# First modulation of a hybrid retention, attention and expert block: in quarters over four column groups

## The chip, the cores and the metric

The kernel runs on one core of a Trainium2 chip. The metric is the device time of one execution in microseconds (us); less is better. The engines are PE (TensorE, matmuls), DVE (VectorE), ACT (ScalarE), POOL (GpSimd) and SP (SyncE, which issues most DMAs). All data are float32.

## What is computed

The block takes 256 latent tokens `x` and 256 context tokens `ctx` of width 1024, a vector `c` for the latent rows and one `c_ctx` for the context rows. What matters here is its beginning:

```python
def ada_mod(cvec, w, b):
    m = jax.nn.silu(cvec) @ w + b          # w is 1024 x 6144
    return jnp.split(m[:, None, :], 6, axis=-1)

def modulate(t, shift, scale):
    return t * (1.0 + scale) + shift

h_lat = modulate(rms_norm(x, norm1_g), m_lat[0], m_lat[1])
h_ctx = modulate(rms_norm(ctx, norm1_g), m_ctx[0], m_ctx[1])
zl = split_proj(h_lat @ w_in)              # w_in is 1024 x 8896
zc = split_proj(h_ctx @ w_in)
```

The first 2048 columns of `ada_w` make shift and scale of this first modulation, for both kinds of rows. Of the projection, 384 columns (the latent query rank, "cq"), 320 columns (the key and value rank with its rotary part, "ckv") and 512 columns of a gate ("gm") are computed first. Retention, attention, the merge of both, 32 experts of which each token takes four, and a last norm follow.

## The kernel before, in words

The program is a list of steps, each a function and, where it needs weights, a load (`step`, `run_steps`, L205 to L250). Weights are loaded by SP into a ring of 7 tiles (`WR`), so a load is issued when the step seven loads earlier has used its tile. Each engine runs its instructions in the order in which the steps were written. A float32 product of a weight block is made of three matmuls (`mm3`, L282): the weights are split into a high part (ACT, L274) and the rest (DVE, L275), and so are the modulated rows, `hh` (ACT, L379) and `hl` (DVE, L381, from `hf`, which DVE or POOL computes, L378).

The beginning, in steps:

- `ada_half(0)`: for each of 8 row blocks k of `ada_w`, one load of 128 rows by 2 x 512 columns (the first 512 shifts and the first 512 scales). Two matmuls with 32 stationary columns (`sT`, of which two are real: silu of `c` and of `c_ctx`), one per column group of PE, add into bank `ap0` (L306). The bias comes as a matmul ahead of the first block (L294).
- Meanwhile the rows of `x` and `ctx` are loaded, squared and summed (ACT, L348), scaled (`norm_rows`, L353, L355) and turned (`xn_transposes`, L143) into `xT`. `keep_warm` (L455) issues small matmuls on ones, of which nothing is used.
- `start1`: `ada_out(0)` copies the sums from `ap0` (L313, L314), `ada_mod(0)` turns them into columns (L320) and makes gain and shift for the first four k (L322, L324); `modulate` follows for those four.
- The cq products for k = 0 to 3, the ckv products for k = 0 and 1, then `ada_half(1)`, 8 more blocks with four small matmuls behind each; `start2` with the same steps for k = 4 to 7; the rest of cq, `cq_norm` (which first clears a 2 MB tile `ada` on POOL, L327), the rest of ckv, `cq_rows` (turning the normed cq, L143), gm, `ckv_norm`, `ckv_rows`, and the gate.

Then the query weights follow in three blocks ("up q", 256 columns moving, on `cqh`), the keys and values (on `ckh`), and the rest.

Of the kernel before, what the change touches and what calls it, by code (L numbers as in the profile page):

```python
# [10 lines left out]
F32 = mybir.dt.float32  # L11
# [23 lines left out]
CLK = 60, 6, 4, 10, 20, 20, 16, 8, 16, 16  # L35
# [24 lines left out]
def hybrid_block(ctx: ExitStack, tc: tile.TileContext, A, out, dbg=None):  # L60
# [135 lines left out]


# [13 lines left out]
    def run_steps():  # L211
# [9 lines left out]
        def split_next():  # L221
            w, nk, n, raw = loaded[len(ready)]
            if raw:
                ready.append((w,))
            else:
                ready.append([y[:, :nk * n].rearrange("p (k n) -> p k n", k=nk) for y in split(w[:, :nk * n], nk * n)])
# [9 lines left out]
        for spec, fn in steps:  # L236
            while len(loaded) < min(at[0] + WR, len(loads) - 1):
# [14 lines left out]
    def load(src, r0, nk, pieces, raw=False):  # L252

        n = sum(p[1] for p in pieces)
        w = wtile4()
        v = w[:, :nk * n].rearrange("p (k n) -> p k n", k=nk)
        o = 0
        if len(pieces) > 1 and len({p[1] for p in pieces}) == 1 and nk == 1:
            (c0, cn), (c1, _) = pieces
            a = src[r0:r0 + 128]  # L260
            a = bass.AP(tensor=a.tensor, offset=a[:, c0:c0 + cn].offset, ap=[list(a.ap[0]), [c1 - c0, 2], [1, cn]])
            nc.sync.dma_start(w[:, :n].rearrange("p (c n) -> p c n", c=2), a)
# [5 lines left out]
        return w, nk, n, raw  # L268
# [24 lines left out]
    def ada_bias(ps, r):  # L293
        nc.tensor.matmul(ps, ident[0:12, r:r + 1].to_broadcast([12, 32]), adab, start=True, stop=False)  # L294

    def ada_half(h, ks):
        for k in ks:
            def f(w, k=k):
                if h == 0 and k == 0:
                    bank("ap0")  # L300
                ap0 = B["ap0"]
                for c in range(2):
                    g = 2 * h + c
                    if k == 0:
                        ada_bias(ap0[32 * g:32 * g + 32], 2 * c + h)
                    nc.tensor.matmul(ap0[32 * g:32 * g + 32], sT[:, k], w[:, 512 * c:512 * c + 512],  # L306
                                     start=False, stop=(k == KD - 1))
            step(f, (A["ada_w"][0], 128 * k, 1, [(512 * h, 512), (1024 + 512 * h, 512)], True))

    def ada_out(h):  # L310
        s = slice(64 * h, 64 * h + 64)
        ap0 = B["ap0"]
        nc.vector.tensor_copy(ada0[s, 0:256], ap0[s, 0:256])  # L313
        nc.scalar.activation(ada0[s, 256:512], ap0[s, 256:512], AF.Copy)  # L314

    def ada_mod(h):
        s = slice(64 * h, 64 * h + 64)
        ps = pt_((128, 4, 2, 32))
        for c in range(4):
            nc.tensor.transpose(ps[:, c].rearrange("p a b -> p (a b)"), ada0[s, 128 * c:128 * c + 128], ident[s, s])  # L320
        ks = slice(4 * h, 4 * h + 4)
        nc.vector.scalar_tensor_tensor(mod1[:, 0, :, ks], ps[:, :, 1, 0:2].rearrange("p k r -> p r k"), 1.0,  # L322
                                       g1c[:, None, ks].to_broadcast([128, 2, 4]), op0=OP.add, op1=OP.mult)
        nc.vector.tensor_copy(mod1[:, 1, :, ks], ps[:, :, 0, 0:2].rearrange("p k r -> p r k"))  # L324
# [4 lines left out]

    ada_todo = [(q, k, i) for q in range(2) for k in range(KD) for i in range(2)]  # L330
# [13 lines left out]
    def norm_rows():  # L344
# [4 lines left out]
        r1 = rsqrt(sp, ss, 4, 1.0 / D)  # L349
# [7 lines left out]
    def xn_transposes(u):  # L357
        for k2 in range(KD // 2):
# [6 lines left out]
            if k2 % 2:  # L365
# [20 lines left out]
    def project(pieces, jobs, kks, mid=None, at=None):  # L386

        for k2 in kks:
            def f(hi, lo, k2=k2):
                for k in range(2):  # L390
                    kk = 2 * k2 + k
                    for n, (name, cut, t, a, b, first) in enumerate(jobs):
# [1337 lines left out]
```

## Time and profile before

| | |
|---|---|
| median of 3 runs | 1474.54 us (1474.64, 1470.18, 1474.54) |
| the profiled execution | 1469.68 us, span of its instructions 1467.8 us |
| PE, DVE, ACT busy | 96%, 44%, 24% of the span |
| DMA | 492 MB, mean 335 GB/s |

The stage in question ends near 92 us. A busy PE is not a PE at its peak: matmuls overlap, and a row's duration is longer than the distance to the next one. Where a cost per matmul is wanted, the distance between starts is read.

### The profile page before, as it was taken

To read this page: it belongs to the slowest core of one execution; us is meant where nothing else is said; L and a number is where in the kernel's file an instruction comes from. 1 tells how busy PE (TensorE), PEld (TensorE's weight loads), DVE (VectorE), ACT (ScalarE), POOL (GpSimd) and SP (SyncE) were. 2 spreads that over 40 slices of the span, in tenths; PEclk is the share of its full clock that TensorE was granted. 3 is DMA by queue.
4 is the path that set the end of the run, shared out by engine and by line. 5 is a ranking of instruction groups with operands and counts; after the bars stand their busy time and mean duration, and the time that the engine had idled before them with its cause. 6 is when DMAs were issued, how large, how long until landed. Compare 5 with 4: busy or idle time off the path is not lost.

```text
span 1467.8 us, 18597 instructions
## 1 busy us (share of the span) xinstructions
PE 1405.6 (96%) x7695; PEld 795.8 (54%) x7695; DVE 648.5 (44%) x1113; ACT 348.3 (24%) x605; POOL 72.2 (5%) x84
## 2 busy tenths in 40 slices
PE   8999999999999999999999999999999899999985
PEld 4688888888888764434334334333433343334333
DVE  4488776868675753233233233232222232223224
ACT  4365633534443431101101101101100011001001
POOL 2200050110101000000000000000000000000000
PEclk9999999999999999999999999999999999999998
DMA  8633372654568789999999999999999999999994
GB/s 289 201 120 106 106 270 84 206 169 162 169 205 319 272 338 422 427 427 427 427 427 427 426 428 426 427 427 426 427 427 427 427 427 427 427 428 427 426 422 166
DMA packets 75075, 492.36 MB, mean 335 GB/s; under 512 B 6579, under 2 KB 16892, under 8 KB 50152
## 3 DMA queue, kind: packets, MB, share of 16 engines
q1 hardware_dynamic: 74008, 489.22, 82.9%
q0 software_dynamic: 576, 1.23, 0.3%
q8 instruction: 62, 1.02, 0.3%
q10 hardware_dynamic: 400, 0.66, 0.1%
q14 instruction: 29, 0.24, 0.0%
HBM read 490.03 MB, written 1.05 MB: 335 GB/s over the span
## 4 chain that ended last, share of the span: by engine, by line
PE 55%; DMA 39%; DVE 4%; ACT 1%; issue 1%; POOL 0%; ACTq 0%; DVEq 0%; SPq 0%
DMA w<-in_exp_w_gu_dram 25%; DMA w<-in_exp_w_down_dram 14%; PE ps L1495 12%; PE ps L284 9%; PE ps L285 9%; PE ps L283 9%; PE ps L1526 6%; PE ps L143 2%; PE ps L1354 2%; PE ps L306 1%; PE ps L1442 1%; PE ps L1475 1%; PE ps L455 1%; DVE ws L275 0%; PE ps L1648 0%
## 5 line engine op out<-in xcount | busy, mean ns | idle before, releaser
L1495 PE MATMUL ps<-w,xg 128*64 128x512 f32 x2048 | 459.7, 596 | 32.3 <-DMA w<-in_exp_w_gu_dram 30.5
L1495 PEld LDWEIGHTS ps<-w,xg 128*64 128x64 f32 x2048 | 141.0, 137 | 329.0 <-issue 255.8
L1526 PE MATMUL ps<-w,ga 128*64 128x512 f32 x992 | 218.1, 592 | 0.0
L1482 DVE SCALAR_TENSOR_TENSOR x<-ps,gate,x 128x512 f32<-128x512 f32 x124 | 84.5, 745 | 183.8 <-PE ps L1475 183.8
L275 DVE TENSOR_TENSOR ws<-w,ws 128x1024 fp32r<-128x1024 f32 (+2 forms) x114 | 139.4, 1231 | 57.7 <-ACT ws L274 56.0
L1526 PEld LDWEIGHTS ps<-w,ga 128*64 128x64 f32 x992 | 71.3, 137 | 141.5 <-issue 141.5
L274 ACT ACTIVATE ws<-w 128x1024 fp32r<-128x1024 f32 (+2 forms) x114 | 116.8, 1028 | 90.0 <-PE ps L285 71.6
L1535 DVE TENSOR_TENSOR ps<-ps,gate 128x512 f32<-128x512 f32 (+1 forms) x33 | 22.5, 683 | 259.3 <-PE ps L1526 250.0
L1500 ACT ACTIVATE ps<-ga 128x512 f32<-128x512 f32 x32 | 19.3, 602 | 467.8 <-DVE ga L1499 467.8
L284 PE MATMUL ps<-ws,hh 128*128 128x512 f32 (+3 forms) x304 | 109.8, 361 | 3.7 <-DVE ws L275 3.7
L283 PE MATMUL ps<-ws,hh 128*128 128x512 f32 (+3 forms) x304 | 110.3, 363 | 0.1
L285 PE MATMUL ps<-ws,hl 128*128 128x512 f32 (+3 forms) x304 | 109.0, 359 | 0.4 <-DVE hl L381 0.4
L1499 DVE TENSOR_SCALAR ga<-ps 128x512 f32<-128x512 f32 x32 | 22.1, 692 | 159.7 <-PE ps L1495 159.7
L279 ACT ACTIVATE up<-ps 128x512 fp32r<-128x512 f32 (+1 forms) x33 | 19.3, 584 | 258.8 <-DVE ps L1535 258.7
L284 PEld LDWEIGHTS ps<-ws,hh 128*128 128x128 f32 x304 | 57.2, 188 | 14.0 <-DVE ws L275 5.6
L283 PEld LDWEIGHTS ps<-ws,hh 128*128 128x128 f32 x304 | 57.1, 188 | 9.1 <-DVE ptl L280 0.3
L285 PEld LDWEIGHTS ps<-ws,hl 128*128 128x128 f32 x304 | 57.1, 188 | 9.1 <-DVE hl L381 0.7
L1354 PE MATMUL ps<-bgu,ident 128*64 128x512 f32 x256 | 62.0, 605 | 0.0
L338 DVE SCALAR_TENSOR_TENSOR ada<-w,sc,ada 128x1024 f32<-128x1024 f32 x32 | 40.9, 1279 | 0.0
L1515 ACT ACTIVATE ga<-ps 128x512 f32<-128x512 f32 x32 | 19.1, 597 | 73.5 <-PE ps L143 73.5
L284 PE MATMUL ps<-atl,hth 128*128 128x256 f32 x128 | 35.8, 280 | 0.7 <-DVE atl L280 0.7
L1442 PE MATMUL ps<-oh,acc_m 128*128 128x128 f32 x256 | 36.4, 285 | 0.0
(381 smaller groups left out, 1839.5 us busy)
## 6 DMA issues: line engine op xcount, KB each, us to landing
w<-in_exp_w_gu_dram SPq DMA_DIRECT2D x124, 2048.0 KB, 39.1
w<-in_exp_w_down_dram SPq DMA_DIRECT2D x62, 2048.0 KB, 39.1
w<-in_ada_w_dram SPq DMA_DIRECT2D x48, 512.0 KB, 5.7
w<-in_w_in_dram SPq DMA_DIRECT2D x48, 512.0 KB, 4.8
w<-in_w_in_dram SPq DMA_DIRECT2D x32, 256.0 KB, 4.3
w<-in_w_branch_ret_dram SPq DMA_DIRECT2D x16, 512.0 KB, 4.9
w<-in_exp_w_gu_dram SPq DMA_DIRECT2D x8, 1024.0 KB, 27.3
w<-in_w_branch_mla_dram SPq DMA_DIRECT2D x8, 512.0 KB, 5.1
```

The source lines that it names most:

```text
L143: nc.tensor.transpose(dst, src, ident[:n, :n])
L274: nc.scalar.activation(hi[:, :n], src, AF.Copy)
L275: nc.vector.tensor_tensor(lo[:, :n], src, hi[:, :n].bitcast(F32), op=OP.subtract)
L283: nc.tensor.matmul(ps, a[0], b[0], start=start, stop=False, skip_group_check=True)
L284: nc.tensor.matmul(ps, a[0], b[1], start=False, stop=False, skip_group_check=True)
L285: nc.tensor.matmul(ps, a[1], b[0], start=False, stop=stop, skip_group_check=True)
L338: nc.vector.scalar_tensor_tensor(a, w, sc[:, k:k + 1], a, op0=OP.mult, op1=OP.add)
L1354: nc.tensor.matmul(ps[64 * h:64 * h + 64], pick_row(c // 512).to_broadcast([128, CAP]), bgu, start=True, stop=False, skip_group_check=True)
L1442: nc.tensor.matmul(ps[:, i, :w], pairs(part[:, t], 4)[:, k // 2, k % 2], rhs, start=(t + p + i == 0), stop=(t + p == 2), skip_group_check= ...
L1482: nc.vector.scalar_tensor_tensor(a, pss[h], g[:, t:t + 1], a, op0=OP.mult, op1=OP.add)
L1495: nc.tensor.matmul(ps[64 * h:64 * h + 64], xg[k // 4][:, k % 4, sl], w[:, c:c + 512], start=False, stop=(k == KD - 1), skip_group_check=True)
L1526: nc.tensor.matmul(py[64 * h:64 * h + 64], hT[f], w[:, 1024 * r + 512 * h:1024 * r + 512 * h + 512], start=(f == 0), stop=(f == KD - 1))
```

## The change

The first modulation is computed in quarters instead of halves. A quarter is 256 shifts and 256 scales, that is two k of the rows. Its 8 row blocks go round four column groups (block kk to group kk % 4) and so leave four partial sums; `sel`, a 128 by 2 matrix of ones and zeros, adds them up in the matmuls that also turn them into columns. The bias is turned into columns once (`bsc`) and added there. Each load still brings 512 KB, now as two DMAs of 256 KB with rows of 256 columns. The first six loads go into tiles that later stages use (`early_tile`), outside the ring of seven. The cq and ckv products for two k stand between the quarters. The split of the first cq weights comes ahead of the scaling of the rows; the turning of the rows goes by k for both kinds; `ada` is cleared at the program's start; `cq_rows` moves behind the first gm block and `ckv_rows` behind the last.

```diff
-CLK = 60, 6, 4, 10, 20, 20, 16, 8, 16, 16
+CLK = 100, 6, 4, 10, 20, 20, 16, 8, 16, 16
...
 (in gain_cols)
+        bp = pt_((128, 4, 16))
+        for j in range(4):
+            transpose(bp[:, j, 0:12], adab[:, 128 * j:128 * j + 128])
+        for h in range(2):
+            s = slice(4 * h, 4 * h + 4)
+            nc.vector.tensor_copy(bsc[:, 1, s], bp[:, :, h])
+            nc.vector.scalar_tensor_tensor(bsc[:, 0, s], bp[:, :, 2 + h], 1.0, g1c[:, s], op0=OP.add, op1=OP.mult)
...
-            while len(loaded) < min(at[0] + WR, len(loads) - 1):
+            while len(loaded) < len(loads) - 1 and sum(not w[4] for w in loaded[at[0]:]) < WR:
...
-        w = wtile4()
+        w = where() if where else wtile4()
...
+            for k in range(nk):
+                a = src[r0 + 128 * k:r0 + 128 * k + 128]
+                a = bass.AP(tensor=a.tensor, offset=a[:, c0:c0 + cn].offset, ap=[list(a.ap[0]), [c1 - c0, 2], [1, cn]])
+                nc.sync.dma_start(v[:, k].rearrange("p (c n) -> p c n", c=2), a)
...
+    def ada_quarter(q, k2s):
+        for k2 in k2s:
+            def f(w, k2=k2):
+                for k in range(2):
+                    kk = 2 * k2 + k
+                    g = kk % 4
+                    nc.tensor.matmul(B["ap0"][32 * g:32 * g + 32], sT[:, kk], w[:, 512 * k:512 * k + 512],
+                                     start=(kk < 4), stop=(kk >= 4), skip_group_check=True)
+            step(f, (A["ada_w"][0], 256 * k2, 2, [(256 * q, 256), (1024 + 256 * q, 256)], True,
+                     (lambda n=4 * q + k2: early_tile(n)) if 4 * q + k2 < 6 else None))
...
+    def ada_mod(q):
+        ps = pt_((128, 2, 2, 2))
         for c in range(4):
-            nc.tensor.transpose(ps[:, c].rearrange("p a b -> p (a b)"), ada0[s, 128 * c:128 * c + 128], ident[s, s])
+            nc.tensor.matmul(ps[:, c // 2, c % 2], ada0[:, 128 * c:128 * c + 128], sel, start=True, stop=True)
...
+    ada_start()
...
+    def begin(q):
+        ks = range(2 * q, 2 * q + 2)
+        ada_mod(q)
+        if q:
+            ahead[1](0)
+        modulate(0, ks)
+        ahead[1](0 if q == 0 else 1)
+        modulate(1, ks)
...
+    step(lambda: got.__setitem__("r1", norm_factors()))
     step(gain_cols)
+    step(stash("cq"), cq_weights(0))
+    step(lambda: norm_rows(got["r1"]))
+    for k2 in range(3):
+        ada_quarter(0, range(k2, k2 + 1))
+        keep_clock(CLK[1])
+    step(lambda: xn_transposes(0))
+    ada_quarter(0, range(3, 4))
+    step(ada_out)
+    step(lambda: xn_transposes(1))
+    step(lambda: begin(0))
+    step(lambda: bank(*PCQ))
+    for q in range(4):
+        if q:
+            step(stash("cq"), cq_weights(q))
+        if q < 3:
+            step(stash("kv"), kv_weights(q))
+        step(lambda q=q: block(cq_jobs, q, range(2), *got["cq"]))
+        if q == 3:
+            break
+        ada_quarter(q + 1, range(0, 2))
+        if q == 0:
+            step(lambda: (xn_transposes(2), xn_transposes(3), bank(*PKV)))
+        step(lambda q=q: block(kv_jobs, q, range(1), *got["kv"]))
+        ada_quarter(q + 1, range(2, 4))
+        step(ada_out)
+        step(lambda q=q: block(kv_jobs[:2], q, range(1, 2), *got["kv"]))
+        step(lambda q=q: begin(q + 1))
+        step(lambda q=q: block(kv_jobs[2:], q, range(1, 2), *got["kv"]))
...
     step(cq_norm)
-    project_ckv(range(2, 4))
+    step(lambda hi, lo: block(kv_jobs, 3, range(2), hi, lo), kv_weights(3))
+    project_lat(C_GM, ("gm0", "gm1"), range(0, 1))
     step(cq_rows)
-    project_lat(C_GM, ("gm0", "gm1"), range(0, 1))
     step(ckv_norm)
-    project_lat(C_GM, ("gm0", "gm1"), range(1, 3))
+    project_lat(C_GM, ("gm0", "gm1"), range(1, 4))
     step(ckv_rows)
-    project_lat(C_GM, ("gm0", "gm1"), range(3, 4))
```

On PE, at the second half of the modulation, the program before has one pair per row block (L306; between the pairs stand four small matmuls each, not shown). `ap0` is the bank, `sT` the stationary columns, the `w_` tiles hold `ada_w`:

```order
L294 MATMUL ps<-adab,ident 32x512
L306 MATMUL ps<-w_338,sT 32x512
...
L306 MATMUL ps<-w_342,sT 32x512 x2
...
L306 MATMUL ps<-w_527,sT 32x512 x2
L283 MATMUL ps<-ws,hh 128x320
L284 MATMUL ps<-ws,hh 128x320
L285 MATMUL ps<-ws,hl 128x320
L320 MATMUL ps<-ident,ada_164 128x64 x4
```

With the change, the matmuls of the next quarter stand as two fours, one ahead of the first ckv half and one behind it:

```order
L326 MATMUL ps<-w_208,sT 32x512 x2
L326 MATMUL ps<-w_359,sT 32x512 x2
L295 MATMUL ps<-ws,hh 128x320
L296 MATMUL ps<-ws,hh 128x320
L297 MATMUL ps<-ws,hl 128x320
...
L326 MATMUL ps<-w_447,sT 32x512 x2
L326 MATMUL ps<-w_508,sT 32x512 x2
L295 MATMUL ps<-ws,hh 128x320
...
L339 MATMUL ps<-sel,ada_165 128x2 x4
```

So the pairs of one row block each become fours of two loads, and no bias matmul and no small matmul stands between them.

On DVE, at the start, the scaling of the rows came right behind the last step of the norm's factor `rs_y` before:

```order
L158 TENSOR_TENSOR rs_t<-rs_y 128x4
L159 TENSOR_TENSOR rs_t<-rs_t,rs_w 128x4
L160 SCALAR_TENSOR_TENSOR rs_y<-rs_t,rs_y 128x4
L355 TENSOR_SCALAR x_122<-x_122,rs_y 128x1024 x2
L368 COPY xT<-ps 128x2x256 x4
```

With the change six small operations and the split of the first cq weights stand between:

```order
L160 SCALAR_TENSOR_TENSOR rs_y<-rs_t,rs_y 128x4
L194 COPY cols<-ps 128x13
L195 COPY cols<-ps 128x2x4
L202 COPY bsc<-ps 128x4
L203 SCALAR_TENSOR_TENSOR bsc<-ps,cols 128x4
L202 COPY bsc<-ps 128x4
L203 SCALAR_TENSOR_TENSOR bsc<-ps,cols 128x4
L287 TENSOR_TENSOR ws<-w_179,ws 128x768
L380 TENSOR_SCALAR x_122<-x_122,rs_y 128x1024 x2
L393 COPY xT<-ps 128x2x256
L333 COPY ada_165<-ps 128x256
```

On DVE, at the beginning of the second quarter, the order is copy, three small operations, the split of the cq weights, and then the modulated rows:

```order
L333 COPY ada_165<-ps 128x256
L342 TENSOR_TENSOR mod_167<-ps,bsc 128x2x2
L344 TENSOR_TENSOR mod_167<-ps,cols 128x2x2
L346 TENSOR_TENSOR mod_167<-mod_167,bsc 128x2x2
L287 TENSOR_TENSOR ws<-w_204,ws 128x768
L403 TENSOR_SCALAR hf<-xT,mod_167 128x256
L406 TENSOR_TENSOR hl<-hf,hh 128x256 x2
```

This sequence comes three times behind the first quarter, where `start2` had one such sequence for four k.

## Rows read from the trace of the kernel before

**Rows 1.** Busy time in stretches: us, PE, PEld, DVE, ACT, POOL, clock, DMA share, GB/s
```profile
300.00:400.00 100.00, 100.00 (x585) 87.75 (x584) 70.84 (x105) 41.42 (x57) 10.07 (x6) 1.00 0.54 174
600.00:1467.00 867.00, 818.06 (x4298) 333.81 (x4294) 254.01 (x428) 95.22 (x201) 0.00 (x0) 0.99 0.98 416
```
**Rows 2.** The chain that ended last, 25 to 54 us: start, length, what
```profile
25.07 1.84 PE ps L306 x8
...
42.72 0.97 PE ps L294 x2
...
44.99 0.98 PE ps L306 x4
...
52.86 0.98 PE ps L306 x4
```
**Rows 3.** The timeline at the start: start, length, engine, line, operation [idle before]
```profile
5.77 1.88 PE L306 MATMUL ps<-w,sT 128*32 128x512 f32 x2
...
11.27 4.34 PE L455 MATMUL ps<-ones 128*128 128x128 bf16 x60
...
14.72 0.17 DVE L152 TENSOR_SCALAR rs_v<-ss 128x4 f32<-128x4 f32 x1 [10.48 <-ACT junk L348]
...
17.10 1.41 DVE L355 TENSOR_SCALAR x<-x,rs_y 128x1024 f32<-128x1024 f32 x2
...
19.37 1.97 PE L143 MATMUL ps<-ident,x 128*128 128x128 f32 x16
```
**Rows 4.** The timeline of PE: starts nine matmuls apart in cq, sixteen in ckv
```profile
34.02 0.34 PE L285 MATMUL ps<-ws,hl 128*128 128x384 f32 x1
...
35.61 0.34 PE L285 MATMUL ps<-ws,hl 128*128 128x384 f32 x1
...
37.53 0.31 PE L283 MATMUL ps<-ws,hh 128*128 128x320 f32 x1
...
39.87 0.31 PE L284 MATMUL ps<-ws,hh 128*128 128x320 f32 x1
```
**Rows 5.** The timeline of DVE, ACT and POOL around `start2`
```profile
53.90 0.43 DVE L313 COPY ada<-ps 64x256 f32<-64x256 f32 x1 [2.33 <-PE ps L306]
54.36 0.38 ACT L314 ACTIVATE ada<-ps 64x256 f32<-64x256 f32 x1 [3.65 <-DVE ada L313]
55.44 2.08 ACT L379 ACTIVATE hh<-xT,mod 128x256 fp32r<-128x256 f32 x4 [0.70 <-DVE mod L324]
55.58 6.54 POOL L378 TENSOR_SCALAR hf<-xT,mod 128x256 f32<-128x256 f32 x6 [19.87 <-DVE mod L324]
57.17 0.40 DVE L378 TENSOR_SCALAR hf<-xT,mod 128x256 f32<-128x256 f32 x1
58.37 0.95 DVE L275 TENSOR_TENSOR ws<-w,ws 128x768 fp32r<-128x768 f32 x1
61.35 0.42 DVE L381 TENSOR_TENSOR hl<-hf,hh 128x256 fp32r<-128x256 f32 x1 [0.30 <-POOL hf L378]
```
**Rows 6.** The timeline from the end of cq to the keys and values
```profile
63.22 0.49 ACT L538 ACTIVATE t2k<-ps 128x384 f32<-128x384 f32 x1 [0.90 <-PE ps L285]
...
70.50 0.81 PE L143 MATMUL ps<-ident,t2k 128*128 128x128 f32 x6
...
78.58 0.88 DVE L569 TENSOR_SCALAR pth<-ps,rs_y 128x256 f32<-128x256 f32 x2
...
83.69 0.39 PE L283 MATMUL ps<-ws,hh 128*128 128x512 f32 x1
83.92 0.40 PE L284 MATMUL ps<-ws,hh 128*128 128x512 f32 x1
...
91.97 0.40 PE L283 MATMUL ps<-ckh,ws 128*128 128x512 f32 x1
```
**Rows 7.** Busy time in stretches with loads of 256 KB, and of 512 KB
```profile
197.00:205.00 8.00, 8.00 (x36) 6.46 (x35) 5.72 (x7) 3.04 (x3) 3.25 (x7) 1.00 0.82 263
14.00:22.00 8.00, 8.00 (x73) 4.53 (x72) 4.80 (x17) 4.07 (x6) 0.00 (x0) 1.00 1.05 385
```

More of the change, by code (lines that the diff above doesn't have):

```diff
@@ L221, in split_next @@
         def split_next():
-            w, nk, n, raw = loaded[len(ready)]
+            w, nk, n, raw, _ = loaded[len(ready)]
             if raw:
@@ L267, in load @@
                 o += cn
-        return w, nk, n, raw
+        return w, nk, n, raw, where
     def split(src, n):
@@ L291, in bank @@
             B[n] = pt_(shape)
[L293 to L308, printed above, removed]
@@ new lines, in ada_begin, with early_tile @@
+    def ada_begin():
+        bank("ap0")
+        nc.vector.tensor_reduce(sel, ident.rearrange("p (g r) -> p r g", g=4)[:, 0:2], axis=AX.X, op=OP.add)
+    early = {}
+    def early_tile(n):
+        if n % 2 == 0:
+            early[n // 2] = (*first, accp)[n // 2].tile([128, 2, 1024], F32, name=("w", "w", "acc_m")[n // 2])
+        return early[n // 2][:, n % 2]
+    def ada_quarter(q, k2s):
[8 more added lines that the diff above has]
+                     (lambda n=4 * q + k2: early_tile(n)) if 4 * q + k2 < 6 else None))
@@ L355, in norm_rows, with xn_transposes @@
                 nc.vector.tensor_scalar(xt, xt, r1[:, t:t + 1], None, op0=OP.mult)
-    def xn_transposes(u):
-        for k2 in range(KD // 2):
+    def xn_transposes(k2):
+        for u in range(2):
             ps = pt_((128, 2, 256))
@@ L383, in modulate, with project, block @@
                 nc.gpsimd.dma_start(dbg["hT"][:, k, s], hf)
-    def project(pieces, jobs, kks, mid=None, at=None):
+    def project(pieces, jobs, kks):
         for k2 in kks:
[L389 to L392, printed above, removed]
-                        if mid and at == (k, n):
-                            mid()
-                        s = slice(128 * t, 128 * t + 128)
-                        mm3(cut(B[name]), (hh[:, kk, s], hl[:, kk, s]), (hi[:, k, a:b], lo[:, k, a:b]),
-                            start=(kk == 0 and first), stop=(kk == KD - 1))
-            step(f, (A["w_in"][0], 256 * k2, 2, pieces))
+            step(lambda hi, lo, k2=k2: block(jobs, k2, range(2), hi, lo), (A["w_in"][0], 256 * k2, 2, pieces))
+    def block(jobs, k2, ks, hi, lo):
+        for k in ks:
+            kk = 2 * k2 + k
+            for name, cut, t, a, b, first in jobs:
+                s = slice(128 * t, 128 * t + 128)
+                mm3(cut(B[name]), (hh[:, kk, s], hl[:, kk, s]), (hi[:, k, a:b], lo[:, k, a:b]),
+                    start=(kk == 0 and first), stop=(kk == KD - 1))
     def whole(p):
@@ L483, in hybrid_block @@
     step(lambda: bank("spare"))
+    step(ada_begin)
     keep_clock(CLK[0])
[L485 to L502 removed]
+    step(lambda: got.__setitem__("r1", norm_factors()))
+    step(gain_cols)
+    step(stash("cq"), cq_weights(0))
[26 more added lines that the diff above has]
+        step(lambda q=q: block(kv_jobs[2:], q, range(1, 2), *got["kv"]))
     step(lambda: ahead.__setitem__(0, AHEAD))
[L504 removed]
     M = {}
@@ L532, in cq_norm @@
         open_mla()
-        ada_start()
+        ahead[1](1)
         mp = M["mp"]
@@ L557, in ckv_norm @@
     def ckv_norm():
+        ahead[1](2)
         mp = M["mp"]
```

87 lines of the change are left out of this document (27 added, 60 removed).

## The prediction

> **What bounds the kernel now.** I read the busy time in stretches first. From 300 to 400 us PE is busy all the time and the DMA engines half of it; from 600 us to the end the DMA engines are busy for 98% and bring 416 GB/s [rows 1]. The change touches neither stretch. All that follows 92 us is bound to the beginning only by its order (each load waits for a tile, each tile for the step before it), so I take it that whatever the beginning gains or loses shifts the rest by the same time. Then comes the chain that ended last: in the modulation's halves it runs over PE's matmuls on `ada_w`, the last of them at 52.86 [rows 2], and not over a DMA. So the beginning is bound by what PE is given to do, and by the waits of PE for modulated rows. The timelines give the costs.
>
> A single matmul of 512 columns, such as the bias, takes PE 0.97 us for its two instructions, and a pair of them in two column groups 0.98 us [rows 2]: two groups run side by side. The distance between starts, which is what a further matmul costs, is 0.175 us in cq (1.59 us for nine) and 0.147 us in ckv (2.34 us for sixteen) [rows 4], and 0.23 us in gm [rows 6].
>
> **The change, part by part.** All times are on the clock of the profiled execution.
>
> *Start to the first copies.* Before, 512 KB of `ada_w` were loaded ahead of `x` and `ctx`; now they come behind. The factor's chain on DVE began at 14.72, when ACT had squared the last context rows [rows 3]. At the 385 GB/s of rows 7, 0.52 MB are 1.4 us; the first loads run slower than that, so I take 1.6 us, and the chain starts at 13.1. It takes 2.4 us to the scaling, as before (14.72 to 17.10 [rows 3]): 15.5. Six small operations of 0.17 us come next (1.0 us, the price of L152 [rows 3]), then the split of cq weights at 0.95 us (L275 [rows 5]): 17.4. Scaling takes 1.4 us [rows 3]: 18.8, 0.3 us later than before. That the split stands ahead of the norm thus costs what the earlier load gives. The last four transposes (16 took 1.97 us [rows 3]) end at 19.3, and the last pair of the quarter at 20.3. Before, the last pair of the half ended at 26.9 (25.07 and 1.84 [rows 2]). The quarter's loads, 2.1 MB behind 2.5 MB, are there by about 17.5, if 320 GB/s flow from 3 us on (worked out below from rows 7). The 100 small matmuls on ones begin near 4 us. Sixty took 4.34 us [rows 3]; a hundred take 7.2 us at the same pace, and are done before the first two loads of the quarter land (3.0 MB, 12.4 us). They cost nothing, and without that cover the 40 more would cost 2.9 us.
>
> *First block.* From the last pair (53.83) to the first `hh` it took 1.6 us (55.44 [rows 5]). Now there are three small operations on DVE instead of two, and matmuls of two columns in place of transposes, which the trace does not show; at the pace of sixteen transposes in 1.97 us [rows 3] their eight instructions would take 1.0 us. Between nothing and 1.0 us more than before I take 0.5 us, so 2.1 us. The first `hl` is ready 0.9 us behind that (`hf` 0.40, `hl` 0.42 [rows 5]), and twelve cq matmuls take 2.1 us: cq of this quarter is done at 25.4. A four (1.0 us), sixteen transposes (2.0), half of ckv (12 x 0.147 = 1.8) and another four (1.0) end at 31.2. Two of the eight buffers that the transposes fill are copied out by DVE and two by ACT while PE goes on, so I count no wait for them.
>
> *Period of the next quarters.* Count from the end of the second four. DVE copies (0.43), ACT copies behind it (0.38) [rows 5], PE turns, DVE has three small operations (T + 2.1), then the split of cq weights, which now comes ahead of `hf` (0.95: T + 3.0), `hf` and `hl` (0.9): T + 3.9. PE meanwhile has twelve ckv matmuls (1.8), the turning (0.5 to 1.0) and the first cq product, and waits for `hl` some 1.2 us. cq is done at T + 5.7. Four, half of ckv, four: 3.7 more. The period is 9.4 us, so the third quarter's fours end at 40.6, the last at 50.0, and cq at 55.7. Before, cq ended at 63.2 [rows 6].
>
> *Price of a four.* Bounds: 0.98 us, if four groups run side by side as two do, and 1.95 us, if only two run at once. I take 0.98 us, since the pair costs what one matmul costs and shows no loss. The Trainium skill, page "TensorE: Matmul & The Clock Gate", section "Part 3: Packing small matmuls — row/col tiling", gives a speedup of 2.38 for three column tiles, that is 79% of ideal; by that an estimate for a four is 1.2 us, and the six later fours would cost 1.5 us more than by the row. The trace of before has a pair only, at 98% of ideal.
>
> *To the keys and values.* After cq, 24 ckv matmuls (3.5 us) and the first gm block (12 x 0.23 = 2.8 us) end at 62.0; that is 6.3 us behind the end of cq, where it was 7.3 before (63.22 to 70.50 [rows 6]), with the norm and 48 ckv matmuls (7.1 us) side by side. If the norm is slower than PE now, at most 1.0 us is lost; I take none. So the transposes of cq rows start at 62.0 instead of 70.50 [rows 6]: 8.5 us earlier. From there ACT and DVE decide: to the scaled ckv rows it took 8.1 us (78.58 [rows 6]), and the same instructions stand there. Behind them one split of gm weights less stands ahead of the query weights (1 us on ACT, L274). PE before had to do the last gm block there and was late itself; that work is now done beside the norm. The keys and values, at 91.97 before [rows 6], start 9.5 us earlier, with 8.5 and 11 as the ends: the first if ACT and DVE win nothing, the second if PE alone decides and the gm block that it no longer has there counts in full (2.8 us).
>
> *Other edits.* Clearing `ada` (L327) moves to the start of POOL's queue, where POOL has nothing else to do until the first `hf` and DVE waits for `x`: nothing. Six loads go into tiles that are free: nothing. 32 small matmuls between pairs go (six steps from 44.99 to 52.86 [rows 2], 1.31 us each, of which the pair is 0.98: 0.33 us, eight times), and four bias matmuls; both are left out of the sums above.
>
> **Sum.** 9.5 us less than the profiled execution's 1469.68: 1460.2. That execution lies 4.9 us under the median of the three runs, of which two are at 1474.6; a median is to be expected on the same footing, so 1474.54 - 9.5 = **1465.0 us**. About 0.3%, or 4.4 us, is what a measurement of this kernel tells from no change.
>
> **The rivals.**
>
> *Fours do not run four wide.* Six of them cost 0.97 us more each, 5.8 us in all; 3.7 us remain: 1470.8. For it: no row shows more than two groups at once. Against it: two show no loss.
>
> *The loads set the pace, and the kernel is slower.* A quarter needs 2.1 MB of `ada_w` and 0.7 MB of `w_in`, all of it 12.7 MB from 3 us to the last four at 50 us, or 270 GB/s, in loads of 256 KB with 1 KB rows. Such loads (of `w_in`) ran at 263 GB/s with the DMA engines busy for 82%, loads of 512 KB at 385 [rows 7]. So they have some 320 GB/s in them, and the ring is a full quarter ahead. Under 225 GB/s nothing is won; at 200 GB/s the last four ends at 66.5, 16.5 us late, and the time is 1481.5. The Trainium skill, page "DMA: Bandwidth & Descriptors", sections "Anatomy of one DMA — SWDGE (gpsimd) path" and "Bandwidth", asks for loads of at least 1 MB and has a fixed 2 us in each; an estimate by it for loads of 256 KB one at a time is 100 GB/s. Rows 7 disagree, as several are under way at once.
>
> *PE's clock falls at the start.* The first matmuls took 1.88 us each [rows 3], twice the 0.97 of later ones [rows 2], so they ran at 1.2 and not 2.4 GHz; the upper level came with the small matmuls on ones. Now PE has gaps between 11 and 19 us, where it waits for loads and rows. At the lower level until cq the last pair, the transposes and cq would cost 4 us more: 1469.0. Against it: at 25.07 before, four pairs' instructions behind 32 transposes still ran at the upper level (eight in 1.84 us [rows 2]).
>
> *The gain is lost further on.* If a later stage waits for something that does not shift, the time stays near 1474.5. For it: the end is bound by the DMA. Against it: that stream starts when tiles come free, and these shift.
>
> **How the numbers follow.** Forecast 66% (with its own range from 1461 to 1469), fours two wide 12%, loads 6%, clock 7%, gain lost 9%. Faster by over 0.3%: the forecast, the clock, and 5 points of the fours, whose 3.7 us lie just under the bound: 78%. Within 0.3%: the other 7 points and the lost gain, 16%. Slower: the loads, 6%. The range leaves out the lost gain and the loads and takes in the rest, with 2 us below the forecast's best for the two levels of the runs: 1458 to 1472.
>
> **What would show it.** Right: in the new profile a four lasts about 1.0 us; the end of cq lies near 56 us; the transposes of cq rows begin near 62, the keys and values near 82; PE waits some 1.2 us for `hl` in each quarter. Wrong: fours near 2 us, PE idle before a four with a DMA named, early cq matmuls at double distance, or a beginning that is 9 us shorter and an end that is not.

## The result and the profile after

The changed kernel takes 1465.02 us (median of 5 runs, 1464.45 to 1466.82); the runs of before beside it have a median of 1473.3 us (1470.18 to 1474.64). The ratio is 0.9944 with a 95% interval from 0.9924 to 0.9963: 8.3 us less. A later series gave the same: 1465.41 against 1474.56 us, 0.994 (0.9917 to 0.9962).

The profiled executions say less than the medians do. The one of the change took 1464.52 us (span 1462.8), which is near its median; the one of before, 1469.68 us, lies under all five runs of its series. Between these two traces the span differs by 5.0 us, and the stage that the change touches by 5.3 us. So two questions stand: why the stage gave 5.3 and not 9.5 us, and where the medians have the rest from.

The landmarks of the change, as they stand in the timelines of ACT and PE (start, length, operation, idle time before it), are the end of cq, the turning of the cq rows and the first product for the keys:
```profile
60.87 0.49 ACT L571 ACTIVATE t2k<-ps 128x384 f32<-128x384 f32 x1 [0.22 <-POOL hf L403]
66.89 0.82 PE L143 MATMUL ps<-ident,t2k 128*128 128x128 f32 x6
86.66 0.40 PE L295 MATMUL ps<-ckh,ws 128*128 128x512 f32 x1
```
Against [rows 6] these are 2.35, 3.6 and 5.3 us earlier (63.22, 70.50, 91.97). The prediction had 7.5, 8.5 and 9.5. What is missing is missing at the end of cq already. The chain that ended last shows where (start, length, what):
```profile
17.20 1.81 PE ps L326 x4
...
20.33 0.98 PE ps L326 x4
...
31.42 1.05 PE ps L326 x8
...
37.20 0.69 PE ps L297
37.89 0.32 PE ps L295
38.21 0.32 PE ps L296
...
43.54 1.00 PE ps L326 x8
...
48.66 0.44 PE ps L297
49.27 0.18 PE ps L296
...
53.64 1.00 PE ps L326 x8
```
A four takes 1.0 us, as forecast. The second fours end at 32.5, 44.5 and 54.6 us, where 31.2, 40.6 and 50.0 were forecast: the second quarter took 12.1 us and the third 10.1, not 9.4. In the second quarter the cq products stand 0.32 us apart (37.89, 38.21), in the third 0.18. Most of the reason is in the busy times in stretches (us, then PE, PEld, DVE, ACT and POOL, granted clock, DMA share, GB/s):
```profile
14.00:22.00 8.00, 7.62 (x47) 3.28 (x46) 5.28 (x22) 3.09 (x5) 0.00 (x0) 1.00 1.09 350
36.00:41.00 5.00, 4.24 (x19) 3.40 (x19) 2.98 (x7) 1.49 (x3) 2.48 (x2) 0.66 0.69 224
37.00:40.00 3.00, 2.80 (x9) 2.80 (x10) 2.09 (x5) 0.49 (x1) 1.48 (x1) 0.50 0.56 167
```
From 37 to 40 us the granted clock was 0.50, the lower of its two levels (1.2 GHz). Around its fall PE waited three times in the quarter's first products, 1.05 us in all: 0.17 for `hh`, 0.46 for the split weights, 0.42 for `hl`. PE's timeline has these waits in brackets:
```profile
35.44 0.44 PE L295 MATMUL ps<-ws,hh 128*128 128x384 f32 x1 [0.17 <-ACT hh L404]
36.34 0.44 PE L296 MATMUL ps<-ws,hh 128*128 128x384 f32 x1 [0.46 <-DVE ws L287]
37.20 0.69 PE L297 MATMUL ps<-ws,hl 128*128 128x384 f32 x1 [0.42 <-DVE hl L406]
```
The weights were split late only in this quarter. The split on DVE began after a wait of 0.33 us and took 1.21 us, where it took 0.96 us without a wait in the third:
```profile
35.08 1.21 DVE L287 TENSOR_TENSOR ws<-w,ws 128x768 fp32r<-128x768 f32 x1 [0.33 <-DMA w<-in_ada_w_dram]
...
46.78 0.96 DVE L287 TENSOR_TENSOR ws<-w,ws 128x768 fp32r<-128x768 f32 x1
```
So the second quarter's first `hl` product comes 4.7 us behind the last four (32.5 to 37.20), the third's 4.1 us (44.5 to 48.66). Why the split was slow was not tested.

### The profile page after: what moved, and what is told of

Its sections match the earlier page's. It is cut to its first block, busy times and chain, and to the rows that moved or that the text cites. A ratio compares the mean times of both kernels' runs of the same rounds, so it can differ in the third digit from the quotient of the medians.

```text
span 1462.8 us, 18632 instructions
## 1 busy us (share of the span) xinstructions
PE 1398.9 (96%) x7699; PEld 799.7 (55%) x7699; DVE 648.9 (44%) x1128; ACT 348.6 (24%) x607; POOL 73.1 (5%) x84
## 3 DMA queue, kind: packets, MB, share of 16 engines
HBM read 490.03 MB, written 1.05 MB: 336 GB/s over the span
## 4 chain that ended last, share of the span: by engine, by line
PE 56%; DMA 37%; DVE 5%; ACT 1%; issue 1%; SPq 0%; POOL 0%; DVEq 0%; POOLq 0%
DMA w<-in_exp_w_gu_dram 24%; PE ps L1528 14%; DMA w<-in_exp_w_down_dram 11%; PE ps L297 9%; PE ps L295 9%; PE ps L296 9%; PE ps L1559 7%; PE ps L143 2%; PE ps L1387 2%; PE ps L1475 1%; PE ps L1508 1%; DMA w<-in_ada_w_dram 1%; DVE ws L287 1%; DMA ct<-in_router_w_dram 1%; PE ps L326 1%
## 5 line engine op out<-in xcount | busy, mean ns | idle before, releaser
L287 DVE TENSOR_TENSOR ws<-w,ws 128x1024 fp32r<-128x1024 f32 (+1 forms) x114 | 139.6, 1233 | 44.2 <-ACT ws L286 42.4
L286 ACT ACTIVATE ws<-w 128x1024 fp32r<-128x1024 f32 (+1 forms) x114 | 116.7, 1028 | 74.5 <-PE ps L297 71.6
L1533 ACT ACTIVATE ps<-ga 128x512 f32<-128x512 f32 x32 | 19.3, 602 | 466.1 <-DVE ga L1532 466.1
L291 ACT ACTIVATE up<-ps 128x512 fp32r<-128x512 f32 (+1 forms) x33 | 19.3, 584 | 260.4 <-DVE ps L1568 260.3
```

What stands on the lines that cost most here:

```text
L286: nc.scalar.activation(hi[:, :n], src, AF.Copy)
L287: nc.vector.tensor_tensor(lo[:, :n], src, hi[:, :n].bitcast(F32), op=OP.subtract)
```

## The experiments

All times are medians; spans, cq and keys come from the one profiled execution of each run, which can lie far from the median (1470.51 us in the first run below, the highest of its six). "Keys" is the start of the first product of `ckh` (86.66 in the change), "cq" the start of the cq squares (60.87). Where an expectation gives a time for the keys, it means their first split on ACT, 1.6 us behind that product (88.25 us in the change, 93.6 in before).

**The change again.** No edit.

> The change itself once more, next to new runs of the kernel before. In the two profiled executions the first up-projection of keys starts 5.3 us earlier with the change, the span is 5.0 us shorter; the medians differ by 8.3 us, and the profiled execution of before was the lowest of its five. Theory A (the beginning is all there is, before scatters by itself): the new medians differ by 5 to 8.5 us, and before's runs spread again from 1470 to 1475. Theory B (something behind the beginning gained 3 us more, which the profiled execution of before did not show): the medians differ by 8 to 10 us and before's runs lie together near 1473 to 1475. The trace should show cq ending near 60.9 us again and a low granted clock in the second quarter's cq matmuls.

Measured: 1465.41 us (1461.56 to 1470.51) against 1474.56 (1468.84 to 1478.41). The difference of 9.2 us is outside theory A's numbers, while before's spread, nearly 10 us, is as A has it: neither stands as written. This execution had cq at 62.02, the lower clock in the second quarter again, and in the first quarter's cq products too, behind the same wait of 1.15 us for `hh` that the first execution had without it. So the lower clock comes and goes from one execution to the next. Here PE also waited 2.9 us for the router's weights at 483 us, a wait that the profile of before does not have.

**Small matmuls in the wait.**
```diff
...
+        if q:
+            step(lambda: [nc.tensor.matmul(got["ps"][:, 128:256], ones, ones, start=True, stop=True)
+                          for _ in range(10)])
         step(lambda q=q: block(cq_jobs, q, range(2), *got["cq"]))
```
They write into an unused part of the bank of the modulation's columns (that edit of `ada_mod` is not shown).

> The change with ten small matmuls on ones ahead of the cq block in quarters 1 to 3, where PE waits 1.05 us in all for hl; nothing else differs. Theory A (the wait drops the granted clock: 36.4 to 40.3 us at 0.50, so that eleven cq products stand 0.32 us apart in place of 0.16): the clock stays at 1.0, quarter 1's cq takes 1.7 us less, cq ends near 59.2 us instead of 60.9, and the time is 1.7 us under the change's. Rival (the second quarter is late because its weights or the modulated rows come late, the clock is only a companion): cq ends within 0.3 us of 60.9, and the time is the change's. Worse case: the ten small matmuls (0.7 us) delay the first product in each quarter, +0.5 us each.

Measured: 1463.53 us, 1.9 us under the change of the same series, which is inside the scatter of either, so the trace has to tell. (The profiled execution took 1468.93 us, the highest of its six; PE waited 3.88 us for the router's weights in it.) The second quarter, in the same stretch:
```profile
36.00:41.00 5.00, 4.31 (x26) 2.95 (x26) 2.93 (x7) 1.44 (x3) 2.44 (x2) 1.00 0.67 218
```
The clock stays at 1.00 and cq starts at 59.39, 1.5 us earlier than in the change. The rows came no earlier (the first `hl` product at 37.15 us, 37.20 in the change). So the lower clock was worth 1.5 us, and on that Theory A holds. That the small matmuls kept the clock up does not follow from this one execution. The run with the clearing back (below) has none, and the same three waits in its second quarter (0.17, 0.46 and 0.41 us); yet its clock stayed up too, and cq started at 59.18:
```profile
36.00:41.00 5.00, 4.52 (x27) 3.17 (x28) 2.71 (x7) 1.22 (x3) 2.20 (x2) 1.00 0.66 214
```

**Two column groups in place of four.**
```diff
-                    g = kk % 4
+                    g = kk % 2
...
-                                     start=(kk < 4), stop=(kk >= 4), skip_group_check=True)
+                                     start=(kk < 2), stop=(kk >= 6), skip_group_check=True)
```
The copies and the turning then take 64 partitions only.

> The change with the ada_w matmuls in two column groups, not four; the rest as in the change. Theory A (four groups run side by side at no loss: a four took 1.0 us): a four becomes 1.95 us, the six later fours cost 0.95 us more each, 5.7 us in all, cq ends near 66.6 us, time 5 to 6 us over the change's; a little less where PE waited anyway. Rival (the fours stand beside a wait that sets the quarter's pace, loads or rows): cq ends under 63 us, and the time is less than 2 us over the change's.

Measured: 1470.08 us, 4.7 us over the change. PE's timeline, and below it a four of the change:
```profile
27.14 1.91 PE L326 MATMUL ps<-acc_m,sT 128*32 128x512 f32 x8
28.99 1.97 PE L143 MATMUL ps<-ident,x 128*128 128x128 f32 x16
32.65 1.91 PE L326 MATMUL ps<-w,sT 128*32 128x512 f32 x8
```
```profile
31.35 1.07 PE L326 MATMUL ps<-w,sT 128*32 128x512 f32 x8
```
The same eight instructions take 1.91 us, and cq starts at 65.57, 4.7 us later than in the change, though the clock is 1.00 from 36 to 41 us here. The quarter that runs at the upper clock in both shows the price alone: from the third quarter's first `hl` product to the fourth's it takes 11.95 us (51.49 to 63.44) against 10.09 (48.66 to 58.75), 0.93 us for each of its two fours. The forecast had 0.97. The matmuls stand on the path, and this rival of the prediction is refuted.

**More ckv products behind the turning.**
```diff
-        step(lambda q=q: block(kv_jobs, q, range(1), *got["kv"]))
+        step(lambda q=q: block(kv_jobs[:1], q, range(1), *got["kv"]))
         ada_quarter(q + 1, range(2, 4))
         step(ada_out)
-        step(lambda q=q: block(kv_jobs[:2], q, range(1, 2), *got["kv"]))
+        step(lambda q=q: block(kv_jobs[1:3], q, range(1), *got["kv"]))
         step(lambda q=q: begin(q + 1))
-        step(lambda q=q: block(kv_jobs[2:], q, range(1, 2), *got["kv"]))
+        step(lambda q=q: block(kv_jobs[3:], q, range(1), *got["kv"]))
+        step(lambda q=q: block(kv_jobs, q, range(1, 2), *got["kv"]))
```


> The change with nine of the twelve ckv products of a quarter's first row block moved behind the second four: six beside the copies of the modulation, three and then the twelve of the second block behind the turning, where PE waits for hl. Counted in steps of 0.147 us: ahead of the four 3 x 0.147 in place of 12, behind the turning 15 in place of 6, that is 1.3 us more cover against a wait of 1.05 us. Theory A (after a quarter's last four the rows are what PE waits for): each of three quarters gets 1.0 us shorter, the second one by the clock's 1.7 us more; cq ends near 56 us, and the time is 3 to 5 us under the change's. Rival (the second four then waits for its loads, which come only a quarter ahead): PE waits for a DMA before the fours, cq ends over 60 us, the time is within 1 us of the change's.

Measured: 1462.36 us, 3.05 us under the change; cq at 56.96, keys at 82.72. PE waits 0.26 us for `hl` in the second quarter, and not in the third and fourth. In this execution the first quarter's products ran at the lower clock (0.62 from 24 to 28 us), behind a wait of 1.16 us for `hh`. The later quarters' fours did not wait for their loads. Theory A holds: the rows set the pace, and work put into that wait is free.

**The tail as before.**
```diff
-    project_lat(C_GM, ("gm0", "gm1"), range(0, 1))
     step(cq_rows)
+    project_lat(C_GM, ("gm0", "gm1"), range(0, 1))
     step(ckv_norm)
-    project_lat(C_GM, ("gm0", "gm1"), range(1, 4))
+    project_lat(C_GM, ("gm0", "gm1"), range(1, 3))
     step(ckv_rows)
+    project_lat(C_GM, ("gm0", "gm1"), range(3, 4))
```


> The change with its last part undone: cq rows turned right behind the last ckv block and ahead of the first gate block (gm0, gm1), the ckv rows turned ahead of the last gate block, as before. In the traces of before and the change the end of cq came 2.35 us earlier (63.22 and 60.87 us), the first split of keys 5.3 us earlier (93.56 and 88.25); so 2.95 us would be the turned order's own gain. Theory A (the turning behind the gate is worth that): keys start near 91.2 us, 2.5 to 3 us later than with the change, the time is 2 to 3 us over the change's. Rival (the quarters let ACT and DVE do their norm earlier, the order is worth nothing): keys start within 0.7 us of 88.25.

Measured: 1467.26 us, on 12 runs from 1463.6 to 1472.0, which tells little. The trace tells more: from cq to the keys it takes 25.91 us (62.24 to 88.15), in the change 25.79, in before 28.75. PE waits 0.79 us for the normed rows, and makes up for it. The turned order is worth 0.1 us between these two executions, and theory A falls.

**The clearing back beside the norm.**
```diff
-    ada_start()
     ada_todo = [(q, k, i) for q in range(2) for k in range(KD) for i in range(2)]
...
         open_mla()
+        ada_start()
         ahead[1](1)
```


> The change with the clearing of ada put back behind the cq norm's start, where POOL clears 16 KB per partition while DVE runs the small operations of the norm; nothing else differs. The prediction took the move for nothing. Theory A (it was nothing): the norm's chain on DVE and the keys' start stand as with the change, keys at 27.4 us behind the end of cq, the time within 1 us of the change's. Rival (POOL's clearing holds DVE, whose first small operation of that norm took 1.31 us beside it before, where others took 0.17): that operation takes over 1 us again, the chain of the norm gets 1.1 to 2 us longer, and so do the keys, if DVE is what they wait for.

Measured: 1467.86 us (1463.83 to 1474.87). From cq (59.18) to the keys (86.77) 27.59 us, 1.8 us more than in the change. DVE in this variant:
```profile
60.66 1.98 DVE L152 TENSOR_SCALAR rs_v<-sq 128x2 f32<-128x2 f32 x1
62.67 0.17 DVE L153 TENSOR_SCALAR rs_b<-rs_v 128x2 int32<-128x2 int32 x1
```
and POOL beside it:
```profile
59.09 3.52 POOL L349 MEMSET ada<- 128x4096 f32 x1
```
In the change the same operation of DVE reads
```profile
62.35 0.16 DVE L152 TENSOR_SCALAR rs_v<-sq 128x2 f32<-128x2 f32 x1
```
and in the kernel before
```profile
64.31 1.31 DVE L152 TENSOR_SCALAR rs_v<-sq 128x2 f32<-128x2 f32 x1 [0.26 <-ACT t2k L538]
```
The operation on 128x2 ends with POOL's clearing (62.64 and 62.61 us). The rival holds: the move that the prediction took for nothing is worth 1.8 us. The Trainium skill, page "SBUF — State Buffer", section "Who interferes with whom", has DVE and GpSimd share one pair of ports, which, where a DVE instruction uses it (a `tensor_scalar` can), one of them holds for a whole instruction; the two rows agree with it.

**The first cq weights behind the first quarter.**
```diff
-    step(stash("cq"), cq_weights(0))
     step(lambda: norm_rows(got["r1"]))
...
     ada_quarter(0, range(3, 4))
+    step(stash("cq"), cq_weights(0))
```


> The change with the load of the first cq weights (393 KB) and their split put behind the first quarter's ada_w loads and matmuls, not ahead of the norm's scaling. Theory A (in the first quarter PE waits for ada_w: its third pair began at 17.20 us behind a DMA, rows were scaled at 18.4 and turned only from 19.28): at 350 GB/s the loads land 1.1 us earlier, the last pair and turning end near 20.3 us (21.3 with the change), all that follows is 1.0 us earlier. Rival 1 (DVE decides, as the prediction took it: the split ahead of the scaling costs 0.95 us): the same 1 us, but then the scaled rows are what PE waits for, with no DMA named ahead of the third pair. Rival 2: the cq weights now come late: PE or DVE waits for w of w_in ahead of the first cq product, and nothing is won or up to 1 us lost.

Measured: 1466.91 us; cq at 61.50. The engines in the first quarter:
```profile
18.33 1.05 PE L326 MATMUL ps<-w,sT 128*32 128x512 f32 x4
19.31 1.09 PE L143 MATMUL ps<-ident,x 128*128 128x128 f32 x8
21.58 1.05 PE L339 MATMUL ps<-sel,ada 128*128 128x2 f32 x8 [1.17 <-DVE ada L333]
```
The loads were what the quarter waited for: the last pair ends at 19.4, not 21.3. But the weights landed at 19.3, their split on DVE ran from 20.23 to 21.19 ahead of the copy of the modulation, PE waited 1.17 us for that copy, and the clock fell behind that wait. A mixture of theory A and rival 2: 1.9 us were won up to the last pair and given back, to that copy and to the clock.

**The router's weights first.** The swap in POOL's queue, at 471 us:
```diff
-        nc.gpsimd.dma_start(O["x"], A["x"].rearrange("o (t p) d -> p (o t) d", p=128))
         O["rw"] = late.tile([128, KD, E], F32, name="ct")
         nc.gpsimd.dma_start(O["rw"].rearrange("p (j r) e -> p j r e", r=2),
                             A["router_w"][0].rearrange("(j p r) e -> p j r e", p=128, r=2))
+        nc.gpsimd.dma_start(O["x"], A["x"].rearrange("o (t p) d -> p (o t) d", p=128))
```


> The change with two DMA issues of POOL's queue swapped, near 471 us: the router's weights ahead of the 1 MB of x. They landed 10.6 us after their issue in the change's profiled execution and 9.3 in that of before; with the change PE waited for them 0.9 us, in other variants 2 to 3.9 us, and not at all before. Theory A (the wait is part of what the earlier beginning does not give to the end, and of the scatter): they land 2 to 4 us earlier, PE waits for no DMA there, the distance from the first split of keys to the router's product is 394.0 us as before, and the median is 1 to 2 us under the change's. Rival (the queue's expert weights hold them, not x): they land 10 us after their issue, only the 0.8 us of the issue is won, and the time is within 0.8 us of the change's.

Measured: 1464.23 us (1463.58 to 1465.62), 1.2 us under the change of the first series, though this execution had the lower clock in two quarters (keys at 88.11). The weights land 7.8 us after their issue, and PE does not wait. Theory A holds, with the smaller gain that it allowed.

**Before again, for a second profile.** No edit of the kernel before.

> The kernel before itself, for another profile. In forty runs beside the variants it took from 1468.8 to 1481.1 us, while the combined variant, whose trace shows no stretch at the lower clock before its last 15 us, took from 1457.7 to 1458.8. Theory A (before's own scatter is stretches at the lower clock behind waits of PE, and waits for the router's weights; its one profiled execution, at 1469.7 us, had neither): a profile of 1472 us or more shows one or more stretches of 2 to 6 us at a granted clock of 0.5 before 600 us, or a wait for the router's weights of 1 us or more, and the time over 1469.7 is about half of those stretches plus that wait. Rival (the scatter is the stream of expert weights in the last 870 us): the first split of keys starts at 93.6 us, the router's product at 487.5, and all the time over 1469.7 is lost behind 545 us.

Measured: the profiled execution took 1475.33 us, span 1473.4, 5.6 us over the first. Its keys start at 92.12, 0.15 us later than in the first. Then, in PE's timeline, come a wait and, further on, transposes that stand 5.8 us later than the same ones of the first profile, shown last:
```profile
490.03 2.55 PE L1226 MATMUL ps<-ct,mod 128*128 128x32 f32 x16 [2.54 <-DMA ct<-in_router_w_dram]
...
506.01 1.04 PE L143 MATMUL ps<-ident,acc_m 128*128 128x128 f32 x8
```
```profile
500.23 1.04 PE L143 MATMUL ps<-ident,acc_m 128*128 128x128 f32 x8
```
In the stretches behind that wait
```profile
484.00:490.00 6.00, 3.49 (x19) 1.68 (x18) 4.13 (x17) 3.83 (x6) 0.00 (x0) 1.00 1.04 398
490.00:498.00 8.00, 7.97 (x29) 6.83 (x30) 1.66 (x3) 0.10 (x1) 0.00 (x0) 0.57 0.58 219
```
In the first profile the product began at 487.54. The wait puts it 2.5 us later, and eight microseconds at a mean clock of 0.57 cost up to 3.4 us: together the 5.8 us at 506 us, and the 5.6 us at the end. A second stretch below full clock (0.72 from 1418 to 1424 us) added at most 0.4 us, which is the growth of the distance behind it. Theory A holds.

**Before with the router's weights first.** The same swap in the kernel before.

> The kernel before with the same swap as in the run with the router's weights first: their DMA ahead of the 1 MB of x in POOL's queue. The second profile of before (1475.3 us) had PE wait 2.5 us for these weights and ran at the lower clock for 7 us behind that wait; the first profile (1469.7) had neither. Theory A (this place is what before's scatter comes from): no wait there, no lower clock before 500 us, the median falls from 1474 to between 1469 and 1471.5 us and lies closer together; then the beginning alone is worth 5 to 7 us, the distance to the change with the same swap (1464.2 us). Rival (the scatter of before has other places too): the median stays over 1472.5 us with runs from 1469 to 1478.

Measured: 1469.73 us (1468.96 to 1470.86) against 1475.83 for before in that series: ratio 0.9957 (0.9939 to 0.9975). The product does not wait:
```profile
487.19 1.87 PE L1226 MATMUL ps<-ct,mod 128*128 128x32 f32 x16
```
From the small matmuls at the start to 1440 us no stretch is at the lower clock. Theory A holds: this one wait, which comes in some executions only, is where before's scatter and most of its median over 1469.7 come from. With the swap in both, change against before is 1464.23 against 1469.73, in two series: 5.5 us between medians, 4.1 between the two profiled spans.

**Combined.** More ckv products behind the turning, the router's weights first, and (the edit of the bank again not shown)
```diff
...
+        if q == 0:
+            step(lambda: [nc.tensor.matmul(got["ps"][:, 128:256], ones, ones, start=True, stop=True)
+                          for _ in range(12)])
         step(lambda q=q: block(cq_jobs, q, range(2), *got["cq"]))
```


> Three edits at once on the change: nine of the first twelve ckv products of a quarter behind its second four (as in the run with more ckv behind, where the keys started at 84.3 us although the first quarter's cq fell to half the clock), twelve small matmuls on ones ahead of the first quarter's cq block, where PE waits 1.15 us, and the router's weights ahead of x. Theory A: no lower clock before 70 us, keys start at 82.4 us or a little later (1.9 us less than 84.3), no wait for the router's weights, span 1374.2 us more than that as before (93.56 to 1467.8): 1456.6, time 1458.4 us. Rival (what is won at the start comes back as a wait further on): keys near 82.4 us, but a new wait behind them and a time over 1461 us.

Measured: 1458.18 us (1457.65 to 1458.83), ratio to before 0.9893 (0.987 to 0.9916): 7 us faster than the change and the fastest version of this study. Its first quarter and the router's product, on PE:
```profile
23.18 0.83 PE L527 MATMUL ps<-ones 128*128 128x128 bf16 x12 [0.32 <-DVE mod L345]
...
26.41 1.07 PE L326 MATMUL ps<-acc_m,sT 128*32 128x512 f32 x8
```
```profile
476.63 1.87 PE L1263 MATMUL ps<-ct,mod 128*128 128x32 f32 x16
```
The clock stays at its upper level from the small matmuls at the start to 1440 us, cq starts at 55.39, keys at 81.16, and no run is more than 0.7 us from the median. The first split of keys stands at 82.75. Theory A holds. Of the three edits, the twelve small matmuls were not run alone, so their own share is not shown.

**Combined, with the first cq weights behind the modulation.** `stash("cq")` of the first quarter stands behind `begin(0)`, which splits these weights as the other quarters do.

> The combined variant (1458.2 us), and the first cq weights' load and split now behind the first quarter's ada_w and behind the three small operations of its modulation, as in the other quarters. In the run where the load alone was moved, the first quarter's last pair of ada_w ended at 19.4 us in place of 21.3, but the split stood ahead of the copy of the modulation, held it until 21.1 us, and the clock fell in that wait. Theory A: with the split out of the copy's way the first modulated rows begin at 21.9 us (combined: 23.0), the first cq product that needs hl starts 0.9 us earlier, keys at 81.8 us (82.7), time 1457.3 us. Rival (the weights, now 1 us later, or the split behind the modulation set the first product): keys at 82.7 us or later, time 1458.2 or more.

Measured: 1460.08 us (1458.65 to 1460.88, 4 runs), cq at 55.56. PE again:
```profile
20.91 0.95 PE L340 MATMUL ps<-sel,ada 128*128 128x2 f32 x8
22.18 0.83 PE L524 MATMUL ps<-ones 128*128 128x128 bf16 x12 [0.32 <-DVE mod L345]
...
24.67 0.44 PE L297 MATMUL ps<-ws,hl 128*128 128x384 f32 x1 [0.75 <-DVE hl L407]
```
The modulation comes 1.0 us earlier than in the combined variant (20.91 against 21.91), and DVE, which has the split now between it and `hl`, gives it back. The rival holds: in both places behind the norm that were tried, DVE's 0.96 us for the split stand on the path. Keys start only 0.17 us later than in the combined variant (81.33), so most of the 1.9 us between the medians come from further on. In this execution the clock was 0.50 from 528 to 534 us, which the combined variant's was not; why it fell stays open.

## Why the prediction was right, and where it was wrong

The time, 1465.0 us, was forecast to the last digit, and faster by over 0.3% was right. The mechanism was right in the main: the beginning got shorter because the products of cq and ckv fill the modulation's time, the fours run four wide, and what the beginning gained (5.3 us in the traces) arrived at the end (5.0 us). But 9.5 us were forecast for the beginning, and a third of what came, 1.8 us, is the work of an edit that was priced at nothing, the clearing of `ada`. That the digits meet is luck, as three errors cancel: the beginning gave 4.2 us too little, the medians have 3 us more from a place that the prediction did not speak of, and the median of before came out 1.2 us lower with five runs than with three. Step by step:

- **Start to the first copies** was mis-sized by 1.0 us. The last pair was to end at 20.3, by the scaling of the rows; it ended at 21.3. The rows were scaled at 18.4, earlier than the 18.8 forecast, but PE was still at the third pair, whose loads set its start at 17.20. So "The quarter's loads [...] are there by about 17.5", which put no wait for them on the path, is what failed. The run with the cq weights behind, which also had their split out of the way, moved that end to 19.4.
- **First block**: 2.3 us to the first `hh` against 2.1, and the second four ended 11.2 us behind the last pair against 10.9. Right.
- **Period of the next quarters**, 9.4 us, is the step that failed most. It was 12.1 in the second quarter and 10.1 in the third, and the end of cq stood 6.2 us behind the last four against 5.7. Each quarter is some 0.7 us longer by small amounts (the modulation ready at T + 2.3, the first `hl` product at T + 4.1, 2.0 us from it to the next four in place of the 1.8 counted). Of the other 2.0 us of the second quarter some 1.5 are the clock, by the run with small matmuls, and 0.6 the late split of its weights. The prediction counted PE's wait for the rows (1.2 us; measured 1.05 in the second quarter, 0.58 in the third) as idle time only, and not as something behind which the clock can fall for the products that follow. It had the clock as a rival at another place, the pairs of the first quarter, with 7% and a price of 4 us. There the trace of the change shows 1.00; in the run with two column groups the clock was at 0.50 from 14 to 17 us, so the rival was possible.
- **Price of a four**: 0.98 us taken, 1.00 measured. The Trainium skill's 2.38 for three column tiles (page "TensorE: Matmul & The Clock Gate", section "Part 3: Packing small matmuls — row/col tiling") would have made 1.2 us; the rows disagree with that estimate.
- **Loads**: 350 GB/s from 14 to 22 us where 320 were assumed; no four waited for its loads behind the first quarter. The rival falls, though in the first quarter one pair did wait (above). The estimate of 100 GB/s from the Trainium skill, page "DMA: Bandwidth & Descriptors", section "Anatomy of one DMA — SWDGE (gpsimd) path", is for loads one at a time and issued from GpSimd; this trace, at 350 GB/s, has several under way, issued from SP.
- **To the keys and values**: 2.0 us were forecast for the stage behind cq, 2.96 came, but not for the reasons given. 1.8 us of it is the clearing of `ada` that no longer holds DVE. The prediction priced that at nothing, although the trace of before has a row for it: L152 takes 1.31 us beside the clearing there, and 0.17 us at the start [rows 3]. The turned order gave 0.1 us. The remaining 1.0 us was not tested by itself; the rows fit the forecast's reason, that PE has less left behind cq, since the turning starts 6.0 us behind the end of cq (66.89) where it was 7.3, and 6.3 were forecast.
- **The sum.** A median was to be expected "on the same footing" as the profiled execution: that failed. The first profile of before had no wait at the router; its runs near the median have one, by the second profile and by the swap, and with the lower clock behind it that is worth 4 to 6 us. In the change the same swap gained 1.2 us only. Why the change loses less there stays open: one of its executions waited 0.9 us for these weights, another 2.9 us, and the profiled execution with the swap had the lower clock in two quarters.

## What to carry to other kernels

A wait of PE costs more than its own length where the clock falls behind it: three waits of together one microsecond cost 1.5 us more in the products that followed. So independent products belong into such waits (3 us less here); a few small matmuls may do as well, which was not shown alone. This holds for waits that no profile at hand shows as costly, since the fall comes in some executions only. Where runs of the same kernel lie 10 us apart, compare two profiles of it before comparing it with another kernel: here one small load behind a large one in POOL's queue was most of that.

## What the runs showed of the hardware

- The clock as a source of scatter. Behind a wait of 1.15 us the granted clock fell to 0.50 for 3 us or so in one execution of the change, and not in another of the same kernel at the same place; behind three waits of 1.05 us in all it fell in the change's second quarter, and did not in the run with the clearing back. Of 23 runs of before beside the combined variant, the five with a mean clock of 0.996 took 1469.0 to 1471.7 us, the three at 0.992 took 1475.2 to 1481.1; the others lie between 1469.9 and 1477.7.
- Four column groups: four 512-column matmuls of 128x32 weights (eight instructions) in 1.00 us, where two groups take 1.85 us for them, from start to start (27.14 to 28.99), and one such matmul alone takes 0.97 [rows 2].
- One operation of DVE on 128x2 elements can take 1.98 us, if POOL clears a large tile meanwhile.
- A load of 128 KB issued from POOL behind one of 1 MB landed after 8.9 to 13.6 us, and after 7.1 to 7.8 us ahead of it.
